# Keys, states and vectors handed over in other layouts, and what the order of the instructions becomes

## The chip, the cores and the metric

The kernel runs on one core of a Trainium2 chip. The metric is device time in microseconds (us), from the launch to the end on that core. The kernel before takes 2627.51 us, the median of 3 runs (2625.67 to 2632.01). How the host lays out inputs and puts outputs back is not in the time; only what the device does is.

## The reference

One step of a decoder layer for 256 prompt tokens and 32 sample tokens (8 sequences of 4 new tokens, each with 2048 tokens in a paged cache), model width 4096. Cut to what matters here:

```python
m = silu(c) @ w_ada + b_ada;  shift, scale, gate = split(m, 3)      # 9 rows of c
h = rmsnorm(x, g_norm) * (1 + scale) + shift
(u_a, v_a, z_a, qkv_b, z_b, a_b, b_b, q_c, k_c, v_c, z_c, qi_c, ki_c, wi_c) = split(h @ w_in)
y_a = chunk_mlp(gelu(u_a), layernorm(gelu(v_a)), a_ws, a_bs) * silu(z_a)
qkv = silu(causal_conv(qkv_b, state_conv, dn_conv_w))               # 4 taps, 6144 channels
o_b, s_new = gated_delta(q, k, v, g, beta, state_dn)                # 16 heads of 128
    # last step of it, per head and sequence: s = s * gl + kg^T @ v_new
idx = top_k(sum_h w_h * relu(q_idx . k_idx), 256)                   # per query token
s = q . cache_k[page, off][idx] / sqrt(128);  p = softmax(s)        # 8 query heads, 2 key heads
o_c = p @ cache_v[page, off][idx]
x = x + gate * (concat(y_a, norm(o_b) * silu(z_b), o_c * silu(z_c)) @ w_out)
```

The kernel does not gather the 256 selected keys. It reads all 2048 keys of each sequence (16 pages of 128 tokens, 2 key heads of 128 features), computes all scores, and adds a large negative number where a key was not selected. All of it is 32-bit.

## The kernel before, in words

**The GEMMs.** The three large products (ada, `h @ w_in`, `mix @ w_out`) keep weights in 128 x 128 pieces in the array and stream 288 token columns past them. A 128 x 512 slice of `w_in` or `w_out` is split in two: ScalarE casts it to `wh`, VectorE subtracts and makes `wl`; TensorE then runs three matmuls of 288 columns per piece (`hH,wh`, `hL,wh`, `hH,wl`), 12 for a slice. Up to 4 slices are split ahead (`N_SPLIT`). The parts of `h @ w_in` come in a fixed list of units.

**The order.** Nothing is scheduled at run time: each engine runs its instructions in the order in which Python wrote them. A `Weaver` (from line 91) decides that order. After each GEMM step, `stages` (line 237) looks through a list of side chains, written as Python generators, and emits a stage of every chain that it believes ready. What it believes is an emission clock of its own: `note` (line 167) and `note_dma` (line 190) add a cost per instruction and keep the time at which every tile is written. A gather issued by GpSimd counts 1.0 us there on GpSimd, plus its bytes, plus 2.0 us until it counts as landed. If the belief is early, the matmul of that stage stands at the head of TensorE's queue and holds up all GEMM work behind it. Every recorded operation has line 74 of the profile (the helper `call` in `Eng`), so the trace is read by tile names.

**The side chains** that the change touches, in the order in which they run:

- Start: `c` (tile `C`) and four small vectors are loaded in rows and turned with transposes (`cT`, `ldT`); the vectors come by five DMAs of GpSimd's queue.
- `idx_sample_gen` (line 1170) makes indices from the page table: `ixk` for keys, `ixv` for values, and scores all cached index keys.
- `topk_gen` (line 1350): 32 rounds of VectorE: `MAX8` finds the next 8 largest of 544 numbers in each of 128 rows (into `LU`), `MATCH_REPLACE8` removes them, and GpSimd copies the 8 in reverse order into `LDn`. One round per stage. From these follows the threshold, and `mneg`, the mask.
- `sample_gen` (line 1432), two halves of 4 sequences. Keys: 16 gathers a half (`gather_k`), each of 128 rows of 4 KB (4 tokens x 2 heads x 128 features); two lanes (`qk_lane`) turn each tile with eight transposes on TensorE (`kT`), copy them out on VectorE and ScalarE (`ktk`), multiply with the queries in eight matmuls (`S`), and copy those scores out on ScalarE. Then mask, softmax, 32 value gathers a half of 128 rows of 2 KB, and the product `so`.
- `conv_gen` for each head of q, k and v: the convolution of the prompt tokens is elsewhere; that of the 32 sample tokens is on GpSimd: first `cv<-xp`, then three times `tap<-xp` and `cv<-cv,tap`, then a copy into `SSG`. `prev_gen` loads the last three rows of before and turns them with 24-wide transposes (`prevT`); `tail_gen` turns the new last rows (`tailT`, `tailo`) and stores them in two DMAs.
- `dn_sample` (line 1971): the delta rule of the sample tokens, for four heads at a time, whose 32 tokens each lie on 32 of the 128 partitions. Its `update` (line 2084) adds `kg^T @ v_new` to the states: for each of the four heads and each four sequences one product `Sup`, 128 x 128 against 512 columns, with `kgm`, in which the rows of the other heads are zero.
- `gmlp_prep` turns the 8 mixing matrices (`wmT`).

From about 2186 us on, only the output projection and the final norm are left.

## Time and profile before

| what | value |
|---|---|
| median of 3 runs | 2627.51 us (2625.67 to 2632.01) |
| the profiled execution: its time | 2626.0 us |
| its span | 2624.3 us |
| mean granted TensorE clock | 0.986 of full speed |
| first key gather to last score of the first half | 897 to 982 us |
| selection rounds | 922 to 1030 us |
| key gathers of the second half to its last score | 1155 to 1225 us |
| output projection and end | 2186 to 2624 us |

Busy shares are a mean over stages with different limits. TensorE's matmuls are pipelined: the time of one in flight (some 300 ns for 288 columns) is more than the distance at which the next follows, so distances are read from the timeline. The list of waits and the "idle before" of a group say what an engine waited for; a wait on an engine other than TensorE only counts where TensorE later waits for it.

### The profile page before, as it was taken

The page shows a single profiled execution, that of the slowest core. Times are in us where ns is not written, and L with a number is a line of the kernel's source. Part 1 is how long each engine was busy: PE and PEld are TensorE (multiplying, and loading weights), DVE is VectorE, ACT ScalarE, POOL GpSimd, SP SyncE. Part 2 cuts the span into 40 slices and gives each one's busy share as a digit, 9 for nine tenths or more (in the row PEclk, how much of TensorE's full clock was granted, in tenths as well). Part 3 has the DMA queues.
Part 4 walks back from the last instruction along what each step waited for, and adds up shares of the span by engine and source line. Part 5 has one row for each costly group of instructions (what it writes and reads, how often), then busy time and mean ns, then how long its engine had stood idle before and what let it go on. Part 6 is the DMA issues. An engine that isn't in the chain of part 4 may idle for free.

```text
span 2624.3 us, 52262 instructions
## 1 busy us (share of the span) xinstructions
PE 2509.4 (96%) x19684; PEld 2245.5 (86%) x19684; DVE 1625.4 (62%) x3633; ACT 1065.7 (41%) x2440; POOL 496.1 (19%) x1137
## 2 busy tenths in 40 slices
PE   5999999999998999999999989999999999999997
PEld 3788888888897888878789969989989989999997
DVE  3477765555578786744458567568576667555554
ACT  4423223333344443334354434444444544444443
POOL 2000000000001232353543343343430210000000
PEclk9999999999999999999999999999999999999998
DMA  7999988888665567677777547577568455655565
GB/s 285 365 336 342 338 318 323 310 318 302 206 197 182 186 225 251 220 274 236 246 238 238 176 154 234 184 216 245 184 203 265 146 195 187 187 180 174 174 188 164
DMA packets 234964, 615.91 MB, mean 235 GB/s; under 512 B 38856, under 2 KB 92348, under 8 KB 234712
## 3 DMA queue, kind: packets, MB, share of 16 engines
q1 hardware_dynamic: 223672, 574.65, 64.7%
q0 software_dynamic: 11040, 37.92, 4.3%
q8 instruction: 155, 2.54, 0.4%
q14 instruction: 97, 0.79, 0.1%
HBM read 587.54 MB, written 24.95 MB: 233 GB/s over the span
## 4 chain that ended last, share of the span: by engine, by line
PE 85%; DMA 7%; DVE 3%; POOL 2%; issue 2%; ACT 1%; SPq 0%; ACTq 0%; DVEq 0%; POOLq 0%
PE acc L74 68%; PE ada L74 7%; DMA kraw<-in_cache_k_dram,ixk 2%; DMA wa<-in_w_ada_t_dram 1%; DMA vraw<-in_cache_v_dram,ixv 1%; PE kT L74 1%; DMA w<-in_w_in_t_dram 1%; PE Sup L74 1%; DVE wl L74 1%; PE YP L74 1%; PE v L74 1%; PE gram L74 1%; PE o L74 1%; POOL vraw L74 1%; PE S L74 1%
## 5 line engine op out<-in xcount | busy, mean ns | idle before, releaser
L74 DVE TENSOR_TENSOR wl<-w,wh 128x512 fp32r<-128x512 f32 (+1 forms) x1216 | 802.2, 681 | 687.4 <-ACT wh L74 680.8
L74 ACT CAST wh<-w 128x512 fp32r<-128x512 f32 (+1 forms) x1216 | 715.0, 611 | 1145.5 <-PE acc L74 860.0
L74 PE MATMUL acc<-hH,wh 128*128 128x288 f32 (+1 forms) x3744 | 1157.7, 309 | 21.0 <-ACT hH L74 8.7
L74 PE MATMUL acc<-hH,wl 128*128 128x288 f32 (+1 forms) x3744 | 1110.2, 297 | 2.0 <-DVE wl L74 1.9
L74 PE MATMUL acc<-hL,wh 128*128 128x288 f32 (+1 forms) x3744 | 1110.7, 297 | 0.5 <-DVE hL L74 0.5
L74 PEld LDWEIGHTS acc<-hH,wh 128*128 128x128 f32 (+1 forms) x3744 | 708.8, 189 | 132.5 <-issue 57.6
L74 PEld LDWEIGHTS acc<-hH,wl 128*128 128x128 f32 (+1 forms) x3744 | 709.2, 189 | 4.8 <-DVE wl L74 4.4
L74 PEld LDWEIGHTS acc<-hL,wh 128*128 128x128 f32 (+1 forms) x3744 | 710.1, 190 | 3.6 <-issue 2.4
L74 PE MATMUL acc<-mL,wh 128*128 128x288 f32 x1024 | 301.8, 295 | 2.4 <-DVE mL L74 2.4
L74 PE MATMUL acc<-mH,wh 128*128 128x288 f32 x1024 | 303.5, 296 | 0.0
L74 PE MATMUL acc<-mH,wl 128*128 128x288 f32 x1024 | 302.1, 295 | 0.0
L74 PEld LDWEIGHTS acc<-mL,wh 128*128 128x128 f32 x1024 | 192.2, 188 | 2.7 <-DVE mL L74 2.7
L74 PEld LDWEIGHTS acc<-mH,wh 128*128 128x128 f32 x1024 | 192.2, 188 | 0.2
L74 PEld LDWEIGHTS acc<-mH,wl 128*128 128x128 f32 x1024 | 192.2, 188 | 0.0
L74 PE MATMUL ada<-wa,cT 128*32 128x512 f32 x1024 | 135.7, 605 | 15.8 <-DMA wa<-in_w_ada_t_dram 15.5
L74 DVE TENSOR_TENSOR zb<-zb,acc 128x288 f32<-128x288 f32 x160 | 70.3, 451 | 41.4 <-PE acc L74 41.2
L74 POOL TENSOR_TENSOR htmp<-yT,gaT 128x32 f32<-128x32 f32 x20 | 7.8, 388 | 449.2 <-ACT wh L74 335.4
L74 PEld LDWEIGHTS ada<-wa,cT 128*32 128x32 f32 x1024 | 28.2, 109 | 72.9 <-issue 54.7
L74 POOL TENSOR_SCALAR frs<-frs 128x1 f32<-128x1 f32 (+1 forms) x3 | 0.9, 297 | 448.2 <-DVE frs L74 448.0
L74 DVE TENSOR_TENSOR R<-R,R 128x248 f32<-128x248 f32 (+30 forms) x248 | 72.4, 292 | 11.6 <-DMA R<-dD 5.0
L74 POOL TENSOR_SCALAR tap<-xp,cwT 128x32 f32<-128x32 f32 x144 | 78.5, 545 | 0.2
L74 POOL DMA_INDIRECT vraw<-in_cache_v_dram,ixv x64 | 66.9, 1045 | 31.7 <-issue 12.4
(462 smaller groups left out, 2395.4 us busy)
## 6 DMA issues: line engine op xcount, KB each, us to landing
w<-in_w_in_t_dram SPq DMA_DIRECT2D x464, 512.0 KB
wa<-in_w_ada_t_dram SPq DMA_DIRECT2D x256, 512.0 KB
w<-in_w_ada_t_dram SPq DMA_DIRECT2D x128, 512.0 KB
w<-in_w_out_t_dram SPq DMA_DIRECT2D x128, 512.0 KB
St<-in_state_dn_dram SPq DMA_DIRECT2D x16, 512.0 KB
out_dram<-St SPq DMA_DIRECT2D x16, 512.0 KB
X<-in_x_prompt_dram SPq DMA_DIRECT2D x8, 512.0 KB
XF<-in_x_prompt_dram SPq DMA_DIRECT2D x16, 256.0 KB
```

The source lines that it names most:

```text
L74: r = f(*a, **k)
```

## The change

- `note_dma`: a gather counts as landed 4.0 instead of 2.0 us after its bytes, for the emission clock only.
- `c`, the four vectors, `state_conv`, `state_dn`, `a_ws` and `cache_k` are handed over in other layouts (features leading). The transposes `cT`, `ldT`, `prevT` and `wmT` go, and their copies out; the vectors are one DMA. The index preparation is shorter: `ixk` is one 128 x 128 operation.
- `topk_gen`: the copies into `LDn` are on ScalarE, and two rounds make a stage.
- `sample_gen`: a key gather now fetches, for one page and one sequence, 128 rows (features) of 1 KB (2 heads x 128 tokens). It needs no transposes (`kT`) and no copies (`ktk`). There are 128 such gathers of 128 KB in place of 32 of 512 KB. A half is eight steps; a step takes two tiles (eight gathers), 16 score matmuls into one bank, and one copy out. The number of score matmuls is the same, 256. Up to four tiles (16 gathers) are in flight.
- The new last rows of the convolution are stored as they lie (`tailT`, `tailo` go; 12 output DMAs for 24); the new states are stored contiguously.
- `update`: `kg` holds only each head's 32 rows; a product uses the 32 rows of one head as a strip of the array (`tile_position`), and two heads' products stand next to each other, in two banks.
- The host puts two outputs back in the reference's layout.

```diff
-        self.used(self.parts, out, e + 2.0, "D")
+
+        self.used(self.parts, out, e + (4.0 if key == "G" else 2.0), "D")
...
+    vecs = const([P, 321], "vecs")
+    bT, gnT, onT = vecs[:, 0:96], vecs[:, 96:128], vecs[:, 320:321]
+    cwT = vecs[:, 128:320].rearrange("p (j c) -> p j c", j=4)
...
-    dma(C[0:8], I["c_prompt"].rearrange("r (s c) -> (r s) c", c=512))
-    dma(C[8:72], I["c_sample"].rearrange("r (s c) -> (r s) c", c=512))
+    C = tl("xp", [P, KT * 9], "C")
+    dma(C, I["c_t"])
...
+    dma(vecs, I["vecs_t"])
+    th = tl("xp", [P, KT * 9], "cth", 1)
+    A.activation(th, C, AF.Tanh, scale=0.5)
+    V.scalar_tensor_tensor(C, th, 1.0, C, op0=OP.add, op1=OP.mult)
+    V.tensor_scalar(cT[:, 0:KT * 9], C, 0.5, None, op0=OP.mult)
...
-        X.ixk = tl("ap", [P, 2, 16], "ixk", 1, I32)
-        for hf in range(2):
-            V.tensor_scalar(ptf[:, 1 + hf:2 + hf], ptf[:, 1 + hf:2 + hf], 32.0, sub16, op0=OP.mult, op1=OP.add)
-            V.tensor_scalar(X.ixk[:, hf], iof, ptf[:, 1 + hf:2 + hf], None, op0=OP.add)
+        X.ixk = tl("ap", [P, P], "ixk", 1, I32)
+        V.tensor_scalar(X.ixk, ptF, 128.0, iop[:, 0:1], op0=OP.mult, op1=OP.add)
...
-            G.tensor_copy(LD_[:, n], mx)
+            A.copy(LD_[:, n], mx)
             cur = W1
-            yield
+            if n % 2:
+                yield
...
-        k_rows = I["cache_k"][0].rearrange("n (e l) h d -> (n e) (l h d)", e=32)
+        k_rows = I["cache_k_t"].rearrange("n d h k -> (n d) (h k)")
...
-            raw = tl("ap", [P, 4, 256], "kraw", 2)
-            G.indirect_dma_start(out=raw.rearrange("p l c -> p (l c)"), out_offset=None, in_=k_rows,
-                                 in_offset=bass.IndirectOffsetOnAxis(ap=X.ixk[:, hf, s:s + 1], axis=0))
+        def gather_k(hf, j):
+
+            raw = tl("ap", [P, 4, 2, P], "kraw", 2, tag="kt" if j % 2 else "kraw")
+            for bb in range(4):
+                i = 16 * (4 * hf + bb) + j
+                G.indirect_dma_start(out=raw[:, bb].rearrange("p h k -> p (h k)"), out_offset=None, in_=k_rows,
+                                     in_offset=bass.IndirectOffsetOnAxis(ap=X.ixk[:, i:i + 1], axis=0))
...
-            raws = [gather_k(hf, 0), gather_k(hf, 1)]
-
-            def qk_lane(par):
-                raw = raws[par]
-                for s in range(par, 16, 2):
-                    yield [raw]
-                    yield from bank(2)
-                    pk = [pr4("kT") for _ in range(2)]
-                    for kv in range(2):
-                        for l in range(4):
-                            T.transpose(pk[kv][:, l], raw[:, l, kv * HD:(kv + 1) * HD], ident)
-                    if s + 2 < 16:
-                        raw = gather_k(hf, s + 2)
-                    yield [pk[1]]
-                    kt = tl("ap", [P, 2, 4, P], "ktk", 2, tag="kt")
-                    V.tensor_copy(kt[:, 0], pk[0])
-                    A.copy(kt[:, 1], pk[1])
-                    free(2)
-                    yield from bank()
-                    ps = pr("S")
-                    qk_mm(ps, P, hf, lambda kv, bb: kt[:, kv, :, 32 * bb:32 * bb + 32])
-                    yield
-                    dst = Sk[:, 4 * (s % 4):4 * (s % 4) + 4].rearrange("p l (j u w) -> p l w u j", u=2, w=4)[:, :, s // 4]
-                    for u in range(2):
-                        A.activation(dst[:, :, u], ps[:, 0:P].rearrange("p (l u j) -> p u l j", l=4, u=2)[:, u], AF.Copy,
-                                     scale=HD ** -0.5)
-                    free()
-
-            ls = W.push(qk_lane(0), qk_lane(1), front=True)
-            yield lambda: all(x.done for x in ls)
+            raws = [gather_k(hf, j) for j in range(4)]
+            for s in range(8):
+                two = [raws.pop(0), raws.pop(0)]
+                yield two
+                yield from bank()
+                ps = pr("S")
+                for jj in range(2):
+                    qk_mm(ps[:, jj * P:jj * P + P], P, hf, lambda kv, bb: two[jj][:, bb, kv])
+                if s < 6:
+                    raws += [gather_k(hf, 2 * s + 4), gather_k(hf, 2 * s + 5)]
+                yield
+                A.activation(Sk[:, :, 16 * s:16 * s + 16].rearrange("p c k -> p k c"),
+                             ps[:, 0:2 * P].rearrange("p (k c) -> p k c", c=16), AF.Copy, scale=HD ** -0.5)
+                free()
...
-        c0 = kind * 2048 + g * 512
-        prev = u2k("prev")
-        dma2(prev[0:24], sconv[:, c0:c0 + 512])
-        yield [prev]
-        yield from bank()
-        ps = pr4("prevT")
-        for j in range(4):
-            T.transpose(ps[:, j, 0:24], prev[0:24, j * P:(j + 1) * P], ident[0:24, 0:24])
-        yield
         CV[kind, g] = scT = tl("dnq", [P, 4, 24], "scT", 2)
-        A.copy(scT, ps[:, :, 0:24])
-        free()
-        yield
+        dma2(scT, I["state_conv_t"][4 * kind + g])
+        yield [scT]
...
-        ps = pr4("tailT")
-        for c in range(4):
-            T.transpose(ps[0:27, c], tail[:, c], ident)
-        yield
-        to = u2k("tailo")
-        A.copy(to[0:27], ps[0:27].rearrange("p c n -> p (c n)"))
-        free()
-        yield
-        dma(O[6][0, 0][:, c0:c0 + 512], to[0:3])
-        dma(O[11][0].rearrange("b r c -> (b r) c")[:, c0:c0 + 512], to[3:27])
+        dma(O[6][4 * kind + g], tail)
...
+            dma2(St[hl], I["state_dn_t"][4 * g + hl])
...
-        G.memset(kgm, 0.0)
...
-            V.tensor_scalar(kgm[q, hl], pa[q, 1], sc[q, 2:3], None, op0=OP.mult)
+        V.tensor_scalar(kg, pa[:, 1], sc[:, 2:3], None, op0=OP.mult)
...
-            for hl in range(4):
+
+            for h0 in (0, 2):
                 for b0 in (0, 4):
-                    yield from bank()
-                    pu = pr("Sup")
-                    T.matmul(pu, kgm[:, hl], vk[:, b0:b0 + 4].rearrange("p c n -> p (c n)"), start=True, stop=True)
+                    yield from bank(2)
+                    pus = []
+                    for hl in (h0, h0 + 1):
+                        pus.append(pr("Sup"))
+                        q = slice(32 * hl, 32 * hl + 32)
+                        T.matmul(pus[-1], kg[q], vk[q, b0:b0 + 4].rearrange("p c n -> p (c n)"), start=True, stop=True,
+                                 tile_position=(32 * hl, 0))
                     yield
-                    for b in range(b0, b0 + 4):
-                        i = 8 * hl + b
-                        V.scalar_tensor_tensor(St[hl][:, b], St[hl][:, b], gl[:, i:i + 1],
-                                               pu[:, (b - b0) * P:(b - b0 + 1) * P], op0=OP.mult, op1=OP.add)
-                    free()
-                yield from W.calm()
-                dma(O[10][0, :, 4 * g + hl].rearrange("b d e -> d b e"), St[hl])
+                    for hl, pu in zip((h0, h0 + 1), pus):
+                        for b in range(b0, b0 + 4):
+                            i = 8 * hl + b
+                            V.scalar_tensor_tensor(St[hl][:, b], St[hl][:, b], gl[:, i:i + 1],
+                                                   pu[:, (b - b0) * P:(b - b0 + 1) * P], op0=OP.mult, op1=OP.add)
+                        free()
+                for hl in (h0, h0 + 1):
+                    yield from W.calm()
+                    dma(O[10][4 * g + hl], St[hl])
...
-        wraw = tl("gm", [P, 8, P], "wraw", 1)
-        dma(wraw, I["a_ws"][0].rearrange("h t s -> t h s"))
+        wmT = tl("gm", [P, 8, P], "wmT", 1)
+        dma(wmT, I["a_ws_t"])
...
-        yield [wraw]
-        wmT = tl("gm", [P, 8, P], "wmT", 1)
-        for h4 in range(2):
-            yield from bank()
-            ps = pr4("wmT")
-            for c in range(4):
-                T.transpose(ps[:, c], wraw[:, 4 * h4 + c], ident)
-            yield
-            V.tensor_tensor(wmT[:, 4 * h4:4 * h4 + 4], ps, K.triI[:, None, :].to_broadcast([P, 4, P]), op=OP.mult)
-            free()
+        yield [wmT]
+        V.tensor_tensor(wmT, wmT, K.triI[:, None, :].to_broadcast([P, 8, P]), op=OP.mult)
```

The order of the instructions follows from the emission clock. GpSimd's own order, from before, at the keys of the second half (`kraw` is the gathered tile, `tap`, `cv` and `SSG` are the convolution):

```order
L74 DMA kraw<-in_cache_k_dram,ixk 128x1024
L74 TENSOR_SCALAR cv<-xp,cwT 128x32
L74 TENSOR_SCALAR tap<-xp,cwT 128x32
L74 TENSOR_TENSOR cv<-cv,tap 128x32
L74 DMA kraw<-in_cache_k_dram,ixk 128x1024
L74 TENSOR_SCALAR tap<-xp,cwT 128x32
L74 TENSOR_TENSOR cv<-cv,tap 128x32
L74 TENSOR_SCALAR tap<-xp,cwT 128x32
L74 TENSOR_TENSOR cv<-cv,tap 128x32
L74 COPY SSG<-cv 128x32
L74 DMA kraw<-in_cache_k_dram,ixk 128x1024 x12
```

After, the same place, with one head of the convolution inside it:

```order
L74 DMA kraw<-in_cache_k_t_dram,ixk 128x256 x16
L74 TENSOR_SCALAR cv<-xp,vecs 128x32
L74 TENSOR_SCALAR tap<-xp,vecs 128x32
L74 TENSOR_TENSOR cv<-cv,tap 128x32
L74 DMA kraw<-in_cache_k_t_dram,ixk 128x256 x8
L74 TENSOR_SCALAR tap<-xp,vecs 128x32
L74 TENSOR_TENSOR cv<-cv,tap 128x32
L74 TENSOR_SCALAR tap<-xp,vecs 128x32
L74 TENSOR_TENSOR cv<-cv,tap 128x32
L74 DMA kraw<-in_cache_k_t_dram,ixk 128x256 x8
L74 COPY SSG<-cv 128x32
L74 DMA kraw<-in_cache_k_t_dram,ixk 128x256 x8
```

Twelve gathers stood there in a row, and 16 in all in that half; now there are 64 in the half, each with its own issue, and taps of the convolution stand between groups of eight.

The selection rounds, GpSimd's order before (`LDn` are the copies of the 8 largest):

```order
L74 AFFINE_SELECT segm<-segm 128x128 x3
L74 DMA kraw<-in_cache_k_dram,ixk 128x1024
L74 COPY LDn<-LU 128x8 x2
L74 DMA kraw<-in_cache_k_dram,ixk 128x1024
L74 COPY LDn<-LU 128x8
L74 DMA kraw<-in_cache_k_dram,ixk 128x1024
L74 COPY LDn<-LU 128x8 x2
L74 DMA kraw<-in_cache_k_dram,ixk 128x1024
```

and ScalarE's order after, where these copies stand now, among the casts that the GEMM waits for:

```order
L74 COPY LDn<-LU 128x8 x2
L74 CAST wh<-w 128x512 x2
L74 COPY ptT<-ptp 128x384
L74 COPY LDn<-LU 128x8 x2
L74 CAST wh<-w 128x512
L74 ACTIVATE S<-S 128x16x16
L74 COPY LDn<-LU 128x8 x2
L74 CAST wh<-w 128x512 x2
L74 ACTIVATE S<-S 128x16x16
L74 COPY LDn<-LU 128x8 x2
```

On GpSimd a copy that waited for VectorE held up only gathers; on ScalarE every cast `wh` behind it in the queue waits as well. Between the first and the last `LDn` copy stand 33 casts after the change.

TensorE's order after, at the end of the second half's keys:

```order
L74 MATMUL S<-kraw,qS 32x128 x16
L74 MATMUL acc_14206<-hH_451,wh 128x288
L74 MATMUL acc_14206<-hL_463,wh 128x288
L74 MATMUL acc_14206<-hH_451,wl 128x288
L74 MATMUL S<-kraw,qS 32x128 x16
L74 MATMUL acc_14213<-hH_451,wh 128x288
```

Two steps of scores, eight gathers each, stand three GEMM matmuls apart there. Over the whole second half 291 GEMM matmuls, 128 score matmuls and 12 of ada stand from the first to the last score; before it was 192, 128 and 8, and 112 transposes with them.

## Rows read from the trace of the kernel before

**Rows 1.** The page's head, its first part, and the first row of its fourth part (the chain that ended last, by engine).

```profile
span 2624.3 us, 52262 instructions
PE 2509.4 (96%) x19684; PEld 2245.5 (86%) x19684; DVE 1625.4 (62%) x3633; ACT 1065.7 (41%) x2440; POOL 496.1 (19%) x1137
PE 85%; DMA 7%; DVE 3%; POOL 2%; issue 2%; ACT 1%; SPq 0%; ACTq 0%; DVEq 0%; POOLq 0%
```

**Rows 2.** The view by windows: each row is a stretch in us from the span's start, its length, then the busy us (and instructions) of PE, weight loads, VectorE, ScalarE and GpSimd in it, the mean granted clock of TensorE, the DMA share and GB/s.

```profile
897.00:982.00 85.00, 80.05 (x866) 68.94 (x869) 64.02 (x131) 36.30 (x91) 30.14 (x64) 0.98 0.69 228
1155.00:1225.00 70.00, 64.28 (x678) 56.65 (x677) 29.76 (x55) 29.30 (x72) 24.72 (x35) 0.98 0.76 260
1550.00:2034.00 484.00, 483.76 (x3816) 441.65 (x3815) 333.14 (x833) 223.85 (x605) 164.88 (x405) 1.00 0.69 221
2186.00:2624.30 438.30, 417.64 (x3153) 415.04 (x3151) 239.45 (x424) 180.14 (x316) 3.34 (x6) 0.98 0.57 177
```

**Rows 3.** The groups of TensorE instructions by line and form: how many, their busy us, the mean ns of one in flight, then the idle time of the engine just before them and what ended it.

```profile
L74 PE MATMUL kT<-ident,kraw 128*128 128x128 f32 x256 | 35.2, 283 | 9.6 <-DMA kraw<-in_cache_k_dram,ixk 9.4
L74 PE MATMUL Sup<-R,R 128*128 128x512 f32 x64 | 35.5, 659 | 3.8 <-DVE St L74 3.6
L74 PE MATMUL tailT<-ident,tail 128*27 128x128 f32 x48 | 7.3, 274 | 0.0
L74 PE MATMUL prevT<-ident,prev 24*128 24x24 f32 x48 | 5.0, 220 | 2.1 <-DMA prev<-in_state_conv_dram 2.1
L74 PE MATMUL lg<-kt,QI 64*64 64x128 f32 x256 | 9.1, 276 | 0.0
L74 PE MATMUL YP<-R 128*128 128x128 f32 x192 | 26.1, 276 | 0.0
```

**Rows 4.** The timeline of TensorE in two places, runs of like instructions merged: start us, us, instruction, count. First GEMM matmuls, eight transposes of a key tile and the matmul behind them; then one state-update product (two passes) and what follows it.

```profile
1155.27 0.29 PE L74 MATMUL acc<-hH,wh 128*128 128x288 f32 x1
1155.40 0.30 PE L74 MATMUL acc<-hL,wh 128*128 128x288 f32 x1
...
1162.61 1.09 PE L74 MATMUL kT<-ident,kraw 128*128 128x128 f32 x8 [0.43 <-DMA kraw<-in_cache_k_dram,ixk]
1163.46 0.38 PE L74 MATMUL acc<-hH,wh 128*128 128x288 f32 x1
...
1533.41 1.02 PE L74 MATMUL Sup<-R,R 128*128 128x512 f32 x2
1534.27 0.38 PE L74 MATMUL A<-ident,R 128*128 128x128 f32 x2
```

**Rows 5.** The chain of waits at the start of the kernel: start us, us, what.

```profile
10.93 8.80 DMA wa<-in_w_ada_t_dram
```

**Rows 6.** GpSimd's timeline where value gathers stand back to back, one slow gather of the next half, and the groups of key and value gathers over the whole span (columns as in rows 3).

```profile
1103.05 1.03 POOL L74 DMA_INDIRECT vraw<-in_cache_v_dram,ixv  x1 [2.14 <-PE so L74]
1104.38 0.95 POOL L74 DMA_INDIRECT vraw<-in_cache_v_dram,ixv  x1 [0.30 <-issue]
1105.64 0.95 POOL L74 DMA_INDIRECT vraw<-in_cache_v_dram,ixv  x1 [0.31 <-PE acc L74]
...
1223.94 1.43 POOL L74 DMA_INDIRECT vraw<-in_cache_v_dram,ixv  x1 [0.30 <-issue]
...
L74 POOL DMA_INDIRECT kraw<-in_cache_k_dram,ixk x32 | 31.5, 984 | 72.5 <-PE kT L74 32.0 <-PE acc L74 14.7 <-PE kxT L74 10.2
L74 POOL DMA_INDIRECT vraw<-in_cache_v_dram,ixv x64 | 66.9, 1045 | 31.7 <-issue 12.4 <-PE so L74 12.2 <-PE acc L74 2.8
```

**Rows 7.** GpSimd in 1056 to 1314 us by groups, those of the convolution's sample part (columns as in rows 3).

```profile
L74 POOL TENSOR_SCALAR tap<-xp,cwT 128x32 f32<-128x32 f32 x39 | 19.7, 506 | 0.2
L74 POOL TENSOR_TENSOR cv<-cv,tap 128x32 f32<-128x32 f32 x39 | 13.1, 335 | 3.3
L74 POOL TENSOR_SCALAR cv<-xp,cwT 128x32 f32<-128x32 f32 x13 | 5.4, 419 | 34.2 <-ACT tail L74 34.1
L74 POOL COPY SSG<-cv 128x32 f32<-128x32 f32 x12 | 3.9, 322 | 56.2 <-DVE cv L74 56.2
```

**Rows 8.** The selection rounds: VectorE's timeline from 925.1 us; ScalarE's casts between 921 and 1031 us; and from the list of waits, who waited for whom: us in all, times, longest us.

```profile
925.13 0.72 DVE L74 MAX8 LU<-W 128x8 f32<-128x544 f32 x1
925.88 0.09 DVE L74 MATCH_VALUE_LOAD W<-LU,W 128x8 f32 x1
925.96 0.71 DVE L74 MATCH_REPLACE8 W<-LU,W 128x544 f32<-128x544 f32 x1
926.59 0.68 DVE L74 TENSOR_TENSOR wl<-w,wh 128x512 fp32r<-128x512 f32 x1
927.79 0.72 DVE L74 MAX8 LU<-W 128x8 f32<-128x544 f32 x1
...
L74 ACT CAST wh<-w 128x512 fp32r<-128x512 f32 x43 | 26.3, 619 | 37.9 <-PE acc L74 31.7 <-DMA w<-in_w_in_t_dram 3.8 <-DVE W L74 2.2
...
POOL LDn L74 <- DVE LU L74: 60.4, 26, 8.3
```

**Rows 9.** The view by windows around one wait of TensorE, columns as in rows 2.

```profile
1178.40:1181.90 3.50, 1.19 (x10) 0.99 (x9) 0.88 (x2) 0.59 (x1) 0.94 (x1) 0.99 1.01 404
1181.90:1185.30 3.40, 3.40 (x26) 2.65 (x27) 0.69 (x1) 0.58 (x1) 0.93 (x1) 0.50 0.32 130
```

**Rows 10.** The list of waits in 2034 to 2230 us (us in all, times, longest): TensorE's for the input of the output projection.

```profile
PE acc L74 <- DVE mL L74: 2.4, 1, 2.4
```

91 lines of the change are left out of this document (24 added, 67 removed), and 4 rows, old and new, of the table _OUTS.

## The prediction

> **What bounds the kernel now.** I read the page's first part and its chain first. TensorE is busy 2509.4 us of 2624.3 and has 85% of the chain; what is lost is about 115 us of waits and a clock a little under full [rows 1]. So an instruction taken off TensorE is worth its full distance to the next one, as long as nothing else becomes late. The view by windows says where that holds: between 1550 and 2034 us TensorE is busy 483.76 of 484 us, but at the two halves of the keys it already waits 5 of 85 and 6 of 70 us, while VectorE, ScalarE and GpSimd are each well under full [rows 2]. The groups and the timeline give prices and distances [rows 3, 4], the groups of GpSimd the gathers [rows 6]. Engines run in order, so a stage emitted before its data are there stops the GEMM; the question is what the new order asks of GpSimd and ScalarE.
>
> **What goes from TensorE.** Eight key transposes begin at 1162.61 and the matmul behind them at 1163.46 [rows 4]: 0.85 us, 0.106 each. 256 of them [rows 3] are 27.1 us. The 48 tail transposes are of the same kind (5.1 us); the 48 smaller ones of the old convolution rows I take at 0.08 between nothing and 0.106 (3.8 us); 8 of the mixing matrices and some 8 of `c` and the vectors are 1.7 us. Together 10.6 us. None of it is won at the start: the first ada product waits there for its weights, which land at 19.73 us [rows 5], whatever is prepared before.
>
> **Row strips.** A state product, two passes of 512 columns, takes 0.86 us from its start to the next instruction (1533.41 to 1534.27) [rows 4]; the 64 passes are 32 products [rows 3], 27.5 us. Now two products stand next to each other on different rows of the array. Two side by side in the time of one would save 13.8 us. Not overlapping at all would save 0. The nearest row for work in parts of the array is `lg`, in quarters: 9.1 us for 256, 0.036 each, where `YP`, in the whole array, takes 26.1 for 192, 0.136 [rows 3]; that is a quarter, so parts do overlap here, and at most a pair could also overlap with the next pair: 18. I take 13.8. The gains are then 27.1 + 10.6 + 13.8 = 51.5, say 52 us, and at the least 38.
>
> **The second half's keys (loss D).** A gather takes GpSimd 0.95 us and the next starts 0.30 us after it: from 1104.38 to 1105.64 it is 1.26 us [rows 6]. What it takes does not follow the bytes: key gathers of 512 KB have a mean of 984 ns, value gathers of 256 KB 1045 [rows 6]. So 128 gathers of 128 KB cost GpSimd four times the 32. The emission clock counts 1.0 us for each; here it is 1.25. The order puts all of the 64 of the second half against little GEMM work: from the first score to the last 291 GEMM matmuls at 0.13 us (1155.27 to 1155.40) [rows 4], 38 us, and 140 score and ada matmuls, which I estimate at 0.09, between `lg` and `YP` [rows 3], 13 us: 51 us. At the first score eight gathers must have landed; 56 more must pass until the last, 56 x 1.25 = 70 us, and the taps of four heads of the convolution stand between them. A head is one `cv<-xp`, three `tap`, three `cv<-cv,tap` and a copy: 0.42 + 3 x 0.51 + 3 x 0.34 + 0.32 = 3.3 us [rows 7], 13 us for four. GpSimd needs 83 us, TensorE 51: TensorE waits up to 32 us, or 22 if a further eight gathers had gone out ahead of the first score. I take the middle, 27. Bounds: 0 (GpSimd is far enough ahead), and 45, if four more heads come in between. In the first half no taps stand there: 56 gathers, 70 us, against 414 GEMM matmuls (54 us) and the scores (13), so it costs about nothing.
>
> **The selection rounds (loss E).** A round takes VectorE 1.46 us (925.13 to 926.59) [rows 8]. GpSimd waited 60.4 us for these, in 26 waits [rows 8], and nobody for GpSimd. Now ScalarE does, and the casts `wh` stand behind it. 33 casts lie between the first and the last copy; each slice feeds 12 matmuls of 0.13 us, 1.57 us, so TensorE has 52 us of GEMM there. VectorE needs 32 x 1.46 for the rounds and 33 subtractions `wl` at 0.6 us (two operations in 926.59 to 927.79) [rows 8], 67 us; before, 43 casts in 110 us left room. 15 us are short, 6.3 of them covered by the four slices split ahead: 9 to 15, and I take 12. Bounds 0, and 23 if each of the 16 stages shows one round of 1.46 in full. What comes off VectorE (32 copies `ktk`) makes this no worse in the sum, since they stood earlier.
>
> **The clock (loss F).** After a wait in which TensorE was busy 1.19 of 3.50 us, the next 3.4 us ran at a granted clock of 0.50, the lower level of 1.2 GHz [rows 9], and cost 1.7 us more. New waits bring such stretches: I count six steps of scores that have a wait of several us, and two in the selection: 8 x 1.7 = 13.6, say 14. Bounds 0 and 24 (14 waits).
>
> **What is given back later (loss G).** The output projection begins when the delta rule has given its last rows. TensorE waits 2.4 us for them [rows 10], so at the end of the delta rule the chain through VectorE and ScalarE is already as late as the GEMM. The strips and the tails take about 24 us from TensorE there, and nothing from VectorE's updates of the states. Not all of the 24 can then be had; I take 10 given back, between 0 and 24. GpSimd's 3.34 us in the last 438 [rows 2] say that nothing else is waited for there.
>
> **The sum.** 27 + 12 + 14 + 10 = 63 against 52: 11 us slower. The profiled execution took 2626.0 us, 1.7 more than its span, and comes out at 2637. The median of the runs, 2627.5, is 1.5 above it, so I forecast 2638.5 us. The change of 4.0 for 2.0 in the emission clock, contiguous states and fewer output transfers I price at nothing: the first only moves stages later (its effect is in the order counted above), and transfers wait for no one in the part where TensorE is busy without gaps [rows 2]; were that cover gone, a state's 512 KB would be waited for a few us in each of four groups.
>
> **A rule on gathers.** One gather in [rows 6] takes 1.43 us in place of 0.95, while the means stay at 0.98 and 1.05: slow ones are few. The Trainium skill, page "SBUF — State Buffer", section "🔬 SBUF: two separate sides", says that some VectorE operations hold the port pair shared with GpSimd for a whole instruction, and that GpSimd then cannot write the descriptors of its transfers. By that rule gathers beside VectorE's casts and copies would all be late; the means of this trace do not bear that out, the slow one may be such a case.
>
> **Rivals.**
> - GpSimd keeps up (the other side, faster). If the 0.30 us between gathers are no cost of its own, a gather is 0.95: 56 x 0.95 + 13 = 66 us against 51 with 8 to 10 of lead, so D is 7; E is 8, F two waits (3), G 10. 28 against 52: 24 us faster, 2603.5. It decides where a gather takes no more than (51 + 10 - 13) / 56 = 0.86 us: from there D is nothing. For it: GpSimd has 45 us free of 70 in that window [rows 2]. Against it: in both places with gathers back to back the gap is there, at 1.26 [rows 6].
> - The waits just eat the gain. D at its lower 22, E 9, F five waits (8.5), G 10: 49.5 against 52, 2625. For it: each loss stands at its lower working. Against: it needs all of them low at once.
> - Every gather as slow as the slow one: 1.43 + 0.30 in place of 1.25, 56 x 0.48 = 27 us more in the second half alone: 2665.5. For it: more gathers at VectorE's busy stretches. Against: the means of [rows 6].
> - The row strips do not overlap: 13.8 more, 2652.
>
> **How the numbers follow.** The forecast has 0.40, with a range of its own of 2630 to 2650. GpSimd keeps up 0.22; gain eaten 0.20; slow gathers 0.13; strips without overlap 0.05. A measurement tells 0.3%, 7.9 us, from no change, so "same" is 2619.6 to 2635.4. Faster is the first rival and a little of the second: 0.24. Same is most of the second and the low edge of the forecast: 0.22. Slower is the rest: 0.54. The range leaves out part of the first rival below 2600 and part of the third above 2664.
>
> **What would show it.** Key gathers: 128 of about 0.95 to 1.05 us, GpSimd's busy time up by some 95 us. TensorE's waits for `kraw` and those of the GEMM beside them in the second half: 20 to 35 us in sum; if under 10, the first rival holds. ScalarE's waits for `LU`: 30 us or more, with TensorE's wait for `wh` behind them near 12. Windows at 0.50 clock after each. TensorE's busy time near 2509 less 52 plus the slow stretches: about 2470. `Sup` pairs begin within 0.1 us of each other, in half the time. The first matmul of the output projection is at 2186 us or later, although TensorE has less to do. I am wrong if it comes by 2170: then the waits were covered by GEMM that the order moved into them.

## The result and the profile after

The changed kernel takes 2616.22 us, the median of 5 runs (2609.37 to 2617.18), beside 2630.36 us (2625.67 to 2632.10) of the kernel before on the same chip: a ratio of 0.9944 [0.9928, 0.9961]. The forecast was 2638.5 us: 22 us too high, and on the wrong side of no change. That holds for this chip. On another one the unaltered kernel took 2657.02 us, 1.0094 [1.0071, 1.0116]; the last experiments are about that.

The head of the page after and the busy time of the engines (those of before are in [rows 1]):

```profile
span 2614.5 us, 51298 instructions
PE 2483.4 (95%) x19316; PEld 2219.5 (85%) x19316; DVE 1600.1 (61%) x3576; ACT 1036.5 (40%) x2366; POOL 575.0 (22%) x1181
```

TensorE's busy time fell by 26 us, not by the 52 of the sum, and GpSimd's rose by 79. TensorE's mean granted clock went from 0.986 to 0.973. The view by windows, columns as in [rows 2], shows where the clock is lost: the second half of the keys, the first update of the states, and the first 40 us of the output projection, which stood at 1.00 before.

```profile
1131.00:1219.00 88.00, 66.71 (x583) 55.56 (x582) 24.20 (x42) 22.11 (x48) 68.43 (x96) 0.87 0.63 212
1495.00:1519.00 24.00, 18.97 (x50) 8.83 (x49) 13.16 (x50) 10.57 (x51) 10.04 (x27) 0.57 0.23 69
2159.00:2199.00 40.00, 31.56 (x213) 29.75 (x212) 29.32 (x64) 18.53 (x35) 0.00 (x0) 0.87 0.51 169
```

The groups that answer to [rows 3] and [rows 6] (columns as there): the state products now stand on 32 rows, the scores read the gathered keys themselves and wait for them, and there are 128 gathers.

```profile
L74 PE MATMUL Sup<-R,R 32*128 32x512 f32 x64 | 31.2, 870 | 2.8 <-ACT R L74 2.7
L74 PE MATMUL S<-kraw,qS 128*32 128x128 f32 x512 | 25.8, 287 | 16.3 <-DMA kraw<-in_cache_k_t_dram,ixk 16.3
L74 POOL DMA_INDIRECT kraw<-in_cache_k_t_dram,ixk x128 | 128.9, 1007 | 57.8 <-issue 33.5 <-PE S L74 10.5 <-PE kxT L74 7.1
```

And from the list of waits, which answers to [rows 8] (us in all, times, longest): ScalarE now waits for the rounds.

```profile
ACT LDn L74 <- DVE LU L74: 46.9, 32, 5.4
PEld S L74 <- DMA kraw<-in_cache_k_t_dram,ixk: 21.2, 17, 4.0
```

In the second half of the keys (1131 to 1219 us) the same list has a second path to TensorE. ScalarE waits for GpSimd's convolution `cv`, which stands between the gathers, and TensorE waits for the copies `tail` that stand behind that wait on ScalarE:

```profile
ACT cth L74 <- POOL cv L74: 21.0, 3, 12.4
PE S L74 <- DMA kraw<-in_cache_k_t_dram,ixk: 14.4, 14, 3.7
PE acc L74 <- ACT tail L74: 6.9, 1, 6.9
```

By these lists loss E seems confirmed: ScalarE waits 46.9 us where over 30 were forecast. The experiments show that it is the step that failed.

**A balance by places.** The order moves GEMM matmuls across the start of the delta rule, so a start that comes earlier is not yet a gain. I read three instants from each trace: the first transpose `qkT` (the delta rule starts), the fourth group's first `qkT`, and the first matmul of the output projection. To the first I add 0.13 us [rows 4] for each GEMM matmul that was emitted ahead of it more than before; the delta rule is corrected by as much the other way. Gains against before, in us of the profiled executions:

| kernel | `qkT` at | GEMM matmuls ahead | gain up to there | in the delta rule | to the projection | in the projection | sum |
|---|---|---|---|---|---|---|---|
| before | 1314.3 | 6654 | | | | | |
| after | 1305.9 | 6756 | 21.7 | -3.0 | -0.6 | -8.2 | 9.9 |
| old keys (e2) | 1279.1 | 6564 | 23.5 | 6.6 | 1.0 | -9.4 | 21.7 |
| copies on GpSimd (e3) | 1375.7 | 7188 | 8.0 | -26.0 | 1.5 | -9.1 | -25.6 |
| copies alone (e6) | 1285.6 | 6489 | 7.2 | 16.8 | -0.2 | -0.1 | 23.7 |
| two rounds, GpSimd (e9) | 1283.9 | 6468 | 6.3 | 13.3 | 2.5 | -4.8 | 17.3 |
| one round, ScalarE (e10) | 1289.9 | 6528 | 8.0 | 12.8 | 2.5 | -3.0 | 20.3 |
| after, another chip (e16) | 1350.2 | 6756 | -22.6 | 2.8 | 0.8 | -9.4 | -28.4 |

The sums are those of the spans (2624.3 less 2614.5, 2602.7, 2650.1, 2600.5, 2607.0, 2604.0 and 2652.8), within 0.1. The profiled execution of e9 is the second fastest of its twelve, 6 us below their median.

### The profile page after: what moved, and what is told of

Its sections match the earlier page's. It is cut to its first block, busy times and chain, and to the rows that moved or that the text cites. A ratio compares the mean times of both kernels' runs of the same rounds, so it can differ in the third digit from the quotient of the medians.

```text
span 2614.5 us, 51298 instructions
## 1 busy us (share of the span) xinstructions
PE 2483.4 (95%) x19316; PEld 2219.5 (85%) x19316; DVE 1600.1 (61%) x3576; ACT 1036.5 (40%) x2366; POOL 575.0 (22%) x1181
## 5 line engine op out<-in xcount | busy, mean ns | idle before, releaser
L74 PE MATMUL ada<-wa,cT 128*32 128x512 f32 x1024 | 134.1, 607 | 23.8 <-DVE bs L74 18.4
L74 POOL DMA_INDIRECT kraw<-in_cache_k_t_dram,ixk x128 | 128.9, 1007 | 57.8 <-issue 33.5
L74 DVE SCALAR_TENSOR_TENSOR cv<-xp,vecs,cv 128x256 f32<-128x256 f32 x144 | 70.2, 488 | 3.7
```

The source lines that it names most:

```text
L74: r = f(*a, **k)
```

## The experiments

All medians are beside runs of the kernel before on the same chip, and a ratio is to these. The kernels compute the whole reference.

### First: which part carries the gain

Three theories, in this order in the expectations. The first: the strips pay for themselves in granted clock, the handed-over keys win some 20 us, and the copies of the selection cost nothing on ScalarE. The second: moving the copies off GpSimd is itself the gain. The third: the emission clock's price of a gather, 1.0 us, delays the second half. Later ones are told where they come up.

**e1**, the change with the old state update (masked keys in the whole array).

```diff
...
-            for h0 in (0, 2):
+            for hl in range(4):
                 for b0 in (0, 4):
...
-                        T.matmul(pus[-1], kg[q], vk[q, b0:b0 + 4].rearrange("p c n -> p (c n)"), start=True, stop=True,
-                                 tile_position=(32 * hl, 0))
+                    T.matmul(pu, kgm[:, hl], vk[:, b0:b0 + 4].rearrange("p c n -> p (c n)"), start=True, stop=True)
...
```

> The changed kernel, but the state update runs on the whole array again (zero-padded kgm, one bank, one head after the other). Theory 1, the row strips themselves bring the low clock: the stretches of 13.7 us at half clock beside the state updates of groups 1, 2 and 4 (1493 to 1523, 1732, 2114 us) go, the mean clock rises from 0.973 to about 0.98, and the kernel is 5 to 12 us faster than the changed one (2604 to 2611 us), although each pair of products takes 0.7 us more. Rival, the stretches come from waits that other parts of the change made: they stay at their places, the clock stays near 0.973, and the kernel is slower by the 10.7 us that the overlap of 16 pairs saves at full clock (about 2627 us).

Measured: 2610.43 us, 0.9927 [0.9912, 0.9942]. Taking the strips out does not cost the 13.8 us of the sum; it comes out 4 to 6 us faster, with intervals that overlap.

**e2**, the change with the old path of the keys.

```diff
...
-                G.indirect_dma_start(out=raw[:, bb].rearrange("p h k -> p (h k)"), out_offset=None, in_=k_rows,
+            G.indirect_dma_start(out=raw.rearrange("p l c -> p (l c)"), out_offset=None, in_=k_rows,
...
+                            T.transpose(pk[kv][:, l], raw[:, l, kv * HD:(kv + 1) * HD], ident)
...
```

> The changed kernel with the key path of before (32 gathers of 512 KB, transposes, copies, old index preparation); all other edits kept. Theory 1, the new key path won about 20 us, nearly all in the first half (transposes 14 us, waits 5, clock 4) and nothing in the second, where 15 us of new waits and 9 us of low clock eat its 14: about 2636 us. Rival, the step as predicted: GpSimd's time and ScalarE's copies cost more than the transposes save, and this kernel is 10 to 30 us faster than the changed one (2586 to 2606 us).

Measured: 2602.45 us, 0.9894 [0.9878, 0.9909]. So the handed-over keys cost 13 us net; the first theory falls in this point.

**e3**, the change with the copies of the selection back on GpSimd, one round to a stage.

```diff
-            A.copy(LD_[:, n], mx)
+            G.tensor_copy(LD_[:, n], mx)
             cur = W1
-            if n % 2:
-                yield
+            yield
```

> The changed kernel with the copies of the selection rounds on GpSimd again and one round to a stage. Theory 1, on ScalarE they cost TensorE nothing and they had to leave GpSimd because they would stop the gathers behind them: this one is 15 to 35 us slower than the changed one (2631 to 2651 us), with its first half of the keys ending later than 999 us. Rival, the predicted loss of 12 us through casts that wait behind the copies: about 10 us faster (2606 us).

Measured: 2649.80 us, 1.0074 [1.0058, 1.0091], 34 us above the change. That is the largest effect of any part. The second outcome that the last experiments meet is not in it: its list of waits has no row on `remote`, and those of all kernels with that outcome have.

**e4**, the kernel before with the strips alone (the reverse of e1's diff).

> The kernel before with one edit, the row strips of the state update. Theory 1 (strips bring the low clock): the mean clock falls from 0.986 to about 0.975 with new stretches of some 13.7 us beside the updates, and the time is 0 to 8 us above before (2630 to 2638 us). Rival (strips worth their overlap): clock stays near 0.986, 8 to 11 us faster than before (about 2620 us).

Measured: 2629.06 us, 0.9991 [0.9977, 1.0006]: nothing. The strips do overlap. In TensorE's timeline of the change four passes, two products, take 1.06 us up to the next matmul, where one product took 0.86 [rows 4]:

```profile
1910.34 1.13 PE L74 MATMUL Sup<-R,R 32*128 32x512 f32 x4
1911.40 0.40 PE L74 MATMUL acc<-hH,wh 128*128 128x288 f32 x1
```

That saves 0.66 us a pair, 10.6 for 16. But the stretch of the first update has a granted clock of 0.57 in e4 as in the change, and had 0.89 before. First e4, then the kernel before:

```profile
1525.00:1549.00 24.00, 19.41 (x51) 9.19 (x50) 13.05 (x49) 10.77 (x50) 10.71 (x29) 0.57 0.27 75
```

```profile
1525.00:1547.00 22.00, 15.89 (x59) 8.10 (x58) 13.94 (x53) 11.73 (x54) 11.68 (x34) 0.89 0.37 99
```

The last update is at 0.58 in e4 (2136 to 2144 us) and at 0.55 in the change (2113 to 2122), where it was at 0.81 before (2133 to 2142). Between them, where GEMM fills the second and third updates, e4 and the kernel before stand at 1.00.

### Second: the parts against each other

**e5**, e2 and e3 in one. **e6**, the kernel before with the move of the copies alone:

```diff
-            G.tensor_copy(LD_[:, n], mx)
+            A.copy(LD_[:, n], mx)
             cur = W1
-            yield
+            if n % 2:
+                yield
```

**e7**, e1 and e2 in one: the layouts without keys and strips, and the copies. **e8**, the change with the emission clock at 1.25 us for a gather:

```diff
-                     [self.at(x) for x in ins]) + (1.0 if key == "G" else 0.05)
+                     [self.at(x) for x in ins]) + (1.25 if key == "G" else 0.05)
```

> The changed kernel with the key path of before and also the copies of the selection rounds on GpSimd, one round to a stage: what is left of the change are layouts, strips and the emission clock. Theory 2, the move of the copies to ScalarE wins some 20 us by itself, since a copy that waits for VectorE on GpSimd holds up the next gathers and with them the whole sample chain, whatever the size of the gathers: about 2622 us against 2602 with the copies on ScalarE. Rival, with 16 gathers a half GpSimd has time enough, and the move only mattered beside 128 gathers: 2600 to 2607 us.

> The kernel before with one edit, the selection copies on ScalarE and two rounds to a stage. Theory 2: mask ready some 30 us earlier than 1071 us and 12 to 20 us faster (2610 to 2618 us). Rival of the prediction: casts wait behind the copies, 0 to 12 us slower (2630 to 2642 us). Second rival: no difference, since VectorE's rounds set the pace.

> The changed kernel without its two losing parts: key path of before and state update on the whole array. If the two losses found (14 and 6 us) are independent, 2596 us; if the low clock after the updates is there without strips as well, 2602 us or more.

> The changed kernel with one number changed: the emission clock counts 1.25 us for a gather, as measured, in place of 1.0. Theory 3, the loss in the second half comes from scores emitted before their gathers can be there: with the right cost they move behind more GEMM work, the 21 us of waits in the second half fall below 10, and the kernel is 5 to 12 us faster than the changed one (2604 to 2611 us). Rival, the sample chain's own length sets the time, and a later emission only lengthens it: the waits go down, but the time stays or is up to 12 us longer.

Measured: e5 2611.61 us, 0.9935 [0.9916, 0.9954]; e6 2602.34, 0.9901 [0.9879, 0.9924]; e7 2604.64, 0.9912 [0.9890, 0.9933]; e8 2611.17, 0.9945 [0.9924, 0.9965]. Three lines moved into ScalarE's queue are worth 26 us, more than the whole change. From the ratios, in us of 2630, one ladder comes out: copies -26.0 (e6), the other layouts +2.9 (to e7), the strips -4.7 (to e2), the keys +13.2 (to the change), together -14.7. The two steps in the middle are inside the intervals. The parts do not simply add, though: e5 lies between the two times expected, so without the move of the copies the rest already gains 17 us, and the move adds 11 (to e2). The move is worth 26 us alone, 11 beside the other layouts with the old keys, 34 beside the new keys. e8 takes as long as the change (0.9945 and 0.9944), as the rival in its expectation had it: the waits for gathered keys in the second half fall from 14.4 to 3.4 us, but 81 more GEMM matmuls stand ahead of the delta rule, and from there to the projection TensorE stands still 26.0 us in place of 18.4.

Why the copies pay is read in three views. GpSimd's timeline of the kernel before (start us, us, operation, the idle time before it and what ended it): the copies stand between the gathers in one queue, and each waits for a round of VectorE. In none of the traces does an instruction wait for a copy on GpSimd, and the keys behind the copies are not what is late: the last score of the first half comes at 981.1 us before, at 1032.8 in e6, at 992.0 in e3 and at 999.0 in the change.

```profile
969.66 0.19 POOL L74 COPY LDn<-LU 128x8 f32<-128x8 f32 x1 [2.11 <-DVE LU L74]
972.26 0.95 POOL L74 DMA_INDIRECT kraw<-in_cache_k_dram,ixk  x1 [2.41 <-PE acc L74]
974.60 0.19 POOL L74 COPY LDn<-LU 128x8 f32<-128x8 f32 x1 [1.39 <-DVE LU L74]
977.79 0.19 POOL L74 COPY LDn<-LU 128x8 f32<-128x8 f32 x1 [3.01 <-DVE LU L74]
980.49 0.19 POOL L74 COPY LDn<-LU 128x8 f32<-128x8 f32 x1 [2.50 <-DVE LU L74]
982.55 0.19 POOL L74 COPY LDn<-LU 128x8 f32<-128x8 f32 x1 [1.87 <-DVE LU L74]
983.27 0.97 POOL L74 DMA_INDIRECT vraw<-in_cache_v_dram,ixv  x1 [0.53 <-PE acc L74]
```

VectorE's timeline shows when the last round starts and when the mask `mneg`, to which the rounds lead, is made. Before, then e6, then e3:

```profile
1029.11 0.72 DVE L74 MAX8 LU<-W 128x8 f32<-128x544 f32 x1
1070.15 0.72 DVE L74 SCALAR_TENSOR_TENSOR mneg<-W,rank 128x544 bf16<-128x544 f32 x1
```

```profile
1006.18 0.73 DVE L74 MAX8 LU<-W 128x8 f32<-128x544 f32 x1
1042.06 0.72 DVE L74 SCALAR_TENSOR_TENSOR mneg<-W,rank 128x544 bf16<-128x544 f32 x1
```

```profile
1058.39 0.72 DVE L74 MAX8 LU<-W 128x8 f32<-128x544 f32 x1
1104.71 0.72 DVE L74 SCALAR_TENSOR_TENSOR mneg<-W,rank 128x544 bf16<-128x544 f32 x1
```

The mask comes 28.1 us earlier in e6, the start of the delta rule 28.7; with 128 gathers in the queue (e3) both come later than before, by 34.6 and 61.4. What the earlier start buys is GEMM work left for the delta rule, whose chains alone don't fill TensorE. The windows from the start of the delta rule to the output projection (columns as in [rows 2]) of e3, before and e6:

```profile
1376.00:2194.00 818.00, 780.69 (x6001) 705.70 (x6000) 527.37 (x1348) 362.33 (x1017) 249.04 (x623) 0.95 0.59 195
```

```profile
1314.00:2177.00 863.00, 845.63 (x6653) 773.60 (x6652) 577.14 (x1440) 399.27 (x1098) 278.73 (x683) 0.99 0.64 206
```

```profile
1286.00:2154.00 868.00, 862.71 (x6834) 793.03 (x6833) 587.51 (x1454) 407.14 (x1124) 281.38 (x698) 1.00 0.65 211
```

TensorE does nothing in 37.3, 17.4 and 5.3 us of these, and the clock goes 0.95, 0.99, 1.00. More matmuls ahead of the delta rule, fewer in it, more holes in it. How many stand ahead is a matter of the order: a stage of one round counts as done when the emission clock believes all of it done, the copy too, and by that clock a copy on GpSimd comes behind the gathers issued there.

### Third: order or engine, taps, landing

Theory 2 now splits: 2a, the gain is the order (two rounds to a stage); 2b, it is the engine. Theory 4 is that GpSimd's time paces the second half, theory 5 that the landing of 4.0 us in the emission clock costs. Both halves of e6 apart: **e9**, before with two rounds to a stage, copies left on GpSimd; **e10**, before with the copies on ScalarE, one round to a stage.

```diff
-            yield
+            if n % 2:
+                yield
```

```diff
-            G.tensor_copy(LD_[:, n], mx)
+            A.copy(LD_[:, n], mx)
```

> The kernel before, with two selection rounds to a stage, and the copies still on GpSimd. Theory 2a, what wins 26 us is the order: with one round to a stage the next round is emitted only when the clock believes GpSimd's copy done, so two to a stage already give most of it, 2602 to 2612 us. Theory 2b, what wins is the engine (GpSimd's queue, in which the copies and gathers hold each other up): 2624 to 2632 us, as before.

> The kernel before, with the copies on ScalarE, and one round to a stage as before. Theory 2b (the engine): about 2602 us. Theory 2a (the order): 2618 to 2630 us.

Measured: e9 2615.08 us (2608.94 to 2624.88), 0.9959 [0.9945, 0.9974]; e10 2608.72, 0.9930 [0.9914, 0.9946]. Each half gains by itself, 11 us and 18, and together they give 26. That does not set the engine apart from the order, since both edits change the order: 186 (e9) and 126 (e10) fewer GEMM matmuls stand ahead of the delta rule than before. In its first three groups TensorE stands still 3.3 us in e9, 5.0 in e10 and 2.9 in e6, in place of 15.2; ahead of it 75.2, 74.2 and 71.4 us, in place of 76.8. So most is won by GEMM work left for the delta rule, with the copies on either engine, and what the freed queue gives at run time is not shown by itself. The mask is not the measure either: it comes 36 us earlier than before in e9 and 10 in e10.

**e11**, the change with the sample taps of the convolution on VectorE, which takes GpSimd's work from between the gathers of the second half.

```diff
...
-                tap = tl("dnq", [P, NB, NS], "tap", 2)
-                G.tensor_scalar(tap, xs[:, :, w:w + 4], cw_, None, op0=OP.mult)
-                G.tensor_add(ys, ys, tap)
+                V.scalar_tensor_tensor(ys, xs[:, :, w:w + 4], cw_, ys, op0=OP.mult, op1=OP.add)
```

> The changed kernel with the sample taps of the convolution on VectorE (one fused operation for each tap after the first), so that GpSimd has only gathers, small copies and memsets there. Theory 4, GpSimd's time (gathers and taps) sets the pace of the second half's scores: its last score comes 8 us or more earlier than 1217.7, the waits for the gathered keys fall from 16 us to below 10, and the kernel is 5 to 13 us faster than the changed one (2603 to 2611 us). Rival, the waits are for the landing of each gather and not for GpSimd's time: no earlier last score, 2614 to 2620 us.

Measured: 2617.06 us, 0.9967 [0.9956, 0.9979]: no faster. But the place answers. The stretch of the second half's scores in e11, columns as in [rows 2]:

```profile
1123.00:1205.00 82.00, 73.01 (x659) 62.22 (x659) 31.01 (x67) 26.74 (x54) 59.54 (x68) 0.94 0.74 248
```

TensorE's clock is 0.94 there and it stands still 9.0 us; in the change it is 0.87 and 21.3 us (the window 1131:1219 above). The last score comes 13 us earlier, at 1204.7 in place of 1217.7, and the delta rule starts 14.9 us earlier. 81 more GEMM matmuls are emitted by then (6837). But the projection starts only 4.6 us sooner (2154.7 for 2159.3): from the start of the delta rule to there TensorE stands still 36.6 us in place of 18.4. With as many matmuls ahead e8 has 26.0; e11 also gives VectorE some 32 us of taps in that stretch, so the two causes are mixed. GpSimd's time does pace the second half; whether winning time there alone would pay at the end, e11 does not show.

**e12**, e7 with the emission clock's landing time at 2.0 us, as before the change, in place of 4.0.

> The changed kernel with the key path of before, the state update on the whole array, and the emission clock's 2.0 us for the landing of gathers: against the kernel before only the layouts without key path and the copies on ScalarE. Theory 5, the later landing of 4.0 us delays the sample chain and hides what the layouts save: 2592 to 2598 us against 2604.6 with 4.0. Rival, the transposes that the layouts remove were filling waits of the delta rule and are worth nothing: 2601 to 2607 us.

Measured: 2607.86 us, 0.9922 [0.9905, 0.9940], against 0.9912 for e7: not told apart.

### Fourth: the start of the output projection, and other chips

The change, e2 and e3 each lose 8 to 9 us in the projection; the change's chain of waits (start us, us, what) shows where:

```profile
2168.71 7.24 PE acc L74 x53
...
2177.40 0.33 SPq L74
...
2177.78 4.71 DMA mx<-mixD
...
2182.52 1.16 ACT mH L74
...
2183.70 1.37 DVE mL L74
...
2185.11 1.57 PE acc L74 x5
```

The rows of the mixing result are read back (`mx<-mixD`) only after the GEMM ahead has been emitted, so read, cast and rest lie one behind the other, and TensorE stands still 7.7 us. The load waits in the order for `W.calm()`. Theory 6: that wait in the order is the loss. **e13** is the change without that; **e14** is e2 without it; **e15** is e14 with landing 2.0.

```diff
         mx = tl("gm", [P, 4, NTOK], "mx", 2)
-        yield from W.calm()
         dma2(mx, mixD[kb])
```

> The changed kernel with one condition less in the order: the loads of the mixed rows (mx) for the output projection are emitted as soon as a buffer is free, and do not wait until the emission clock believes the weight loads drained. Theory 6, of what the change won before the delta rule, 8 us are lost at the start of the output projection, where TensorE waits 7.7 us for mH, since the load of mx is emitted only when it is needed, and then runs at half clock: the wait falls below 3 us, the stretch from the first to the last matmul of the output projection falls from 436.8 to about 429 us, and the kernel is 6 to 12 us faster than the changed one (2604 to 2610 us). Rival, the wait is for the delta rule itself: it stays, within 3 us of the changed kernel.

> The same edit on the changed kernel with the key path of before (2602.5 us). Theory 6: 2592 to 2597 us, the fastest so far. Rival: 2600 to 2605 us.

> The kernel of the second run here, with the emission clock's landing of gathers at 2.0 us again. If this number of the change is worth nothing by itself, the same time within 4 us of that run; if 4.0 us is what puts the scores behind their gathers, 5 to 10 us slower.

Measured: e13 2644.77 us, 1.0076 [1.0053, 1.0099]; e14 2595.95 (2585.71 to 2600.77), 0.9882 [0.9859, 0.9905]; e15 2589.87, 0.9858 [0.9837, 0.9879], the fastest of all kernels here. The wait for `mH` is gone in all three, and from the first matmul of the projection to the last of the kernel it is 426.0 us in place of 436.8. e14's gain over e2 is 6.5 us by the medians of two chips, with intervals that overlap. e13 was 29 us slower than the change had been: it had run on another chip, though e14 and e15 were fast on that same one. Theory 7: the new order of the keys' first half is open to late loads, and so has two outcomes. On one more chip I ran the change unaltered (**e16**), e13 again (**e17**) and e2 again (**e18**):

> The changed kernel again, unaltered, on the same chip as the next two. Theory 7, the 28 us that e13 was slower come from the order of its first half, which is that of the changed kernel word for word, and which a late weight load can throw back (the copies on ScalarE stand among the casts): then this one is slow too where the next one is, and the distance between the two is 6 to 12 us in favour of e13. Rival, e13's edit itself does it: this one at 2612 to 2618 us, the next at 2640 to 2650.

> e13 again. Theory 7: 6 to 12 us faster than the run before it. Rival: 2640 to 2650 us, with the changed kernel at 2612 to 2618.

> e2 again (the changed kernel with the key path of before). Theory 7: 2600 to 2605 us whatever the other two show, since its first half leaves ScalarE and the weight loads more time. If it moves with them, the key path is not what is open to late loads.

Measured: e16 2657.02 us, 1.0094 [1.0071, 1.0116]; e17 2646.27 (2634.74 to 2649.82), 1.0040 [1.0021, 1.0059]; e18 2604.89, 0.9893 [0.9872, 0.9914]. So it was not the edit that made e13 slow: e17 is 10.8 us faster than e16 beside it. The changed kernel has two outcomes, 41 us apart. The old keys have one (2602.45 and 2604.89), as the kernel before has (2629.66 and 2633.02 on the same two chips). The others with the new keys fit: e1, e8 and e11, on three other chips, stay near the first outcome, and e13, e16 and e17, on two chips, have the second. By the balance above the loss of e16 is all ahead of the delta rule; it arises in the first half of the keys. The same window of both traces, the change first, then e16:

```profile
916.00:1030.00 114.00, 107.47 (x972) 96.33 (x968) 99.69 (x204) 42.43 (x99) 64.92 (x90) 0.97 0.77 265
```

```profile
916.00:1030.00 114.00, 93.45 (x743) 77.07 (x744) 76.24 (x152) 33.61 (x86) 57.09 (x77) 0.88 0.56 185
```

TensorE gets through 743 instructions where it was 972. The list of waits of e16 from 900 to 1040 us has rows that the change's list of the same stretch lacks:

```profile
PE acc L74 <- issue: 10.6, 16, 1.1
ACT wh L74 <- remote: 10.3, 5, 4.1
ACT RL L74 <- remote: 5.4, 1, 5.4
DVE RL L74 <- remote: 4.2, 1, 4.2
```

Engines stand still there for nothing that the trace names, several at a time. Waits on `remote` stand in the lists of all six kernels traced on those two chips, 1.6 to 11.2 us with the old keys and 43 to 69 with the new, and in none of the fourteen others. So what holds the engines comes with the chip, or with the time at which it was used, and the new keys are open to it. A late load of weights, as in theory 7, is neither shown nor excluded: the list of DMA issues of e16 has no time to landing for them. It isn't the gathers: 48 in both windows, mean 974 ns in e16, 968 in the change. What holds the engines was not found. I tried no kernel for it.

## Why the prediction was wrong

**Kernel-wide bound: right, its price not.** TensorE was the engine to watch. But that an instruction taken off it is worth its full distance did not come out in the time.

**Transposes, 27.1 and 10.6: gone from the groups, not seen as a gain.** All of the keys' 27.1 is eaten at once, and 1.8 more: up to the delta rule the change gains 21.7 us, e2 with the old keys 23.5. For the 10.6 of the others, e7 and e12 are 2.9 and 5.5 us slower than the copies alone (e6), inside the intervals; without the move of the copies (e5) layouts, strips and landing time together gain 17.

**Loss D, 27 us: right in place and mechanism, 21 in size.** Forecast was 83 us of GpSimd against 51 of TensorE. From the first score of the second half to the last it is 85.8 us; in these GpSimd is busy 67.2 us and spends 15.9 between gathers, 83 in all. TensorE stands still 21.3 of 88 us, at a mean clock of 0.87. Of the 21.3, 14.4 are waits for gathered keys; the other 6.9 came by a path that the prediction did not have, through ScalarE, which waited for the convolution behind the gathers. In e11, without the taps on GpSimd, that path is gone. What was missing is what follows: the order had put 192 more GEMM matmuls ahead of the delta rule than e2, and those lack later, another 9.6 us in the delta rule. So the keys lose 13 us net, where the sum had them at about zero, or at 10 with the six slow stretches of loss F that it counted there.

The prediction also weighed gathers that are slow beside VectorE, and held them to be few by their mean. The mean of the key gathers is still 1007 ns, 984 before. Sorted one by one, the gathers of keys and values show more. In the change 43 of the 192 overlap no instruction of VectorE, and the longest of these takes 1.04 us; 106 overlap a subtraction `wl`, and 24 of these take over 1.15 us, up to 1.42. The slow one in [rows 6], 1.43 us from 1223.94, ran beside this one of the kernel before:

```profile
1223.87 0.69 DVE L74 TENSOR_TENSOR wl<-w,wh 128x512 fp32r<-128x512 f32 x1 [1.06 <-ACT wh L74]
```

By the Trainium skill, page "SBUF — State Buffer", section "🔬 SBUF: two separate sides", some operations of VectorE hold a port pair shared with GpSimd for a whole instruction, and GpSimd can't write descriptors meanwhile. That some gathers are held up beside VectorE agrees with it; by what they were held no run here shows.

**Loss E, 12 us: the step that failed, in its sign.** The prediction had the casts behind the copies cost 12 us on ScalarE, and put what leaves GpSimd at nothing. But the move of the copies gains 26 us alone (e6) and 11 beside the other layouts (e5 to e2), and put back into the change the copies cost 34 (e3). ScalarE waits 46.9 us for the rounds, as forecast, but TensorE waits for a cast `wh` there only once, 1.9 us: the casts had slack. That GpSimd waited 60.4 us "and nobody for GpSimd" [rows 8] is right of the run, and the wrong thing to ask. The copies had held up the order: a round was emitted only when the emission clock believed the copy on GpSimd done, and so the selection, and the start of the delta rule behind it, stood behind more GEMM work, which was then missing from the delta rule. With two rounds to a stage and the copies left where they were (e9) 11 us are won as well. The working against ScalarE had also left out that the scores gave TensorE another 13 us of cover, 65 in place of 52 against VectorE's 67: by its own rule the shortage was 2 us, not 15.

**Strips, 13.8 us gained: mis-sized.** Overlap is real and worth 10.6 at full clock, by distances; at the end it is worth nothing alone (e4) and between -6 (e1) and +5 (e2 against e7) beside the rest. The updates with strips run at 0.55 to 0.58 in the first group and the last where they had 0.89 and 0.81, and e1, without strips, has 0.85 and 0.71. In the change's third group (1910 to 1930 us) the clock is 1.00 with strips, so they don't lower it everywhere; TensorE had GEMM around each pair there. In its second group it falls to 0.70 (1738 to 1750 us). In e4 nothing but the form of the update was changed, so it is the strips, with the pairing of the products, that lower it where little GEMM stands around them; why, no run here tells.

**Loss F, 14 us: too small.** The clock's mean fell from 0.986 to 0.973, of 2614 us about 34 (0.013 x 2614), waits included. Laid over TensorE's busy time alone, the stretches at half clock in the two traces cost 27.5 us before and 52.4 after, 25 more. The forecast stretches behind waits are there, in the second half of the keys; those in the state updates were not foreseen.

**Loss G, 10 us: right in size, wrong in mechanism.** 8.2 are lost, but in the output projection and by the late read of `mx` (e13, e14 and e17 win it back), not by VectorE's updates. That transfers wait for no one held for the stretch that I had read, and not for this one.

**The sum.** By the ladder the change is -26 for the copies, +13 for the keys and -2 for all else. The forecast had +12, about zero and about zero: two errors, 38 us one way and 13 the other. By the way through e5 it is -17 for layouts, strips and landing time, -11 for the copies and +13 for the keys. The forecast for these, with its eight slow stretches put where it counted them (six in the scores, two in the selection), was -14, +15 and +10: by that way the sign of loss E makes the whole miss. The copies are the largest error by both. The prediction's own sign of being wrong also came: the first matmul of the output projection is at 2159.3 us, ahead of 2170.

## What to carry to other kernels

Before a small operation is priced where it goes, ask what it held up where it was, in the order as well as in the queue: where an emission clock decides the order, a stage can be late because the clock waited for an operation for which no engine waits, and a list of waits does not show that. A stage that starts earlier is worth what the filling work left for the next chain is worth, so compare places only after correcting for work that moved across them. Measure a change on more than one chip before keeping it: here one part decides between two outcomes 41 us apart, and the kernel without it, with the late load moved (e15), is the fastest at 0.9858 [0.9837, 0.9879], though not told apart from e14.

## What was not expected of the hardware

The same program gave 2616 us on one chip and 2657 on another, with engines held for reasons that the trace does not name; the kernel before had medians from 2627.2 to 2633.0. A gather on GpSimd, whose price is 0.95 us, took up to 1.42 beside a subtraction of VectorE. The granted clock stood at 0.57 over 24 us in which TensorE was busy 19.0 with 50 instructions on 32-row strips (the change) and at 0.89 over 22 us in which it was busy 15.9 with 59 (before).
